# Writing the order of the feed-forward part's first and last stages by hand in a two-layer encoder trunk

## The chip, the cores and the metric

The kernel runs on one core of one Trainium2 chip. The metric is the device time of one execution in microseconds, from the first instruction to the last output byte; lower is better. Times are medians of several executions.

## What is computed

Two layers of an encoder trunk over 768 tokens (512 of one request, 256 of another) of width 1024. In each layer four groups of mixers (attention and recurrences) run between two norms, and then the feed-forward part, which the change is about:

```python
for l in range(DEPTH):
    ...
    x = x + _rms(mix, p['norm_mix_post'][l])
    h = _rms(x, p['norm_ffn_pre'][l])
    f = (jax.nn.silu(h @ p['ffn_w_gate'][l]) * (h @ p['ffn_w_up'][l])) @ p['ffn_w_down'][l]
    x = x + _rms(f, p['norm_ffn_post'][l])
return x
```

The inner width of the feed-forward part is 2816: 22 feature tiles of 128.

## The kernel before

All products are made of fp32 values split into a high and a low part (hi and lo), three matmuls for one product: hi by hi, hi by lo, lo by hi. A split takes two instructions: ACT copies the value into the high tile, and DVE or POOL subtracts it from the value for the low tile. hh and hl are the two parts of the normalised input h, transposed; weights come as raw tiles of 128x1024 by DMA (two buffers of tag raw) and are split into wh and wl tiles.

The feed-forward part of a layer has three stages.

*Head.* `ffn` computes feature tiles 0 and 1 directly: `ffn_up(l, f, s)` (L1261) makes the gate and up products of tile f for request s (s=0 is 512 tokens and 96 matmuls, s=1 is 256 tokens and 48 matmuls) into PSUM tiles fg and fu of tag pS, which has two banks. Then ACT takes tanh (L1270), DVE forms the product in two steps, the first reading fg (L1271), the second reading fu (L1272), ACT writes the high part ah (L1273) and DVE the low part al (L1274). `ffn_sums` (L1199) builds, for each of four row pairs k, sums and differences of the two halves of h (t tiles on POOL and DVE) and splits them (ts tiles); the other 20 feature tiles need them, because these are computed by seven block products of half size in the manner of Strassen. `ffn_sums` ends by overwriting the right half of rows 0 to 3 of hh and hl with a difference (L1226, L1227). Then the down projection of tiles 0 and 1 (`down_mm` L1277, six matmuls into a dn tile of tag pa, two banks; `down_add` L1289, an ACT copy into y for the first pair) runs for 6 token tiles by 2 column halves.

*Units.* `ffn_units` (L1296) handles tiles f = 2 to 21. A unit is seven products p of 12 matmuls (`block_mm` L1249), with additions on DVE (L1304), and the preparation of the next tile's weights: splits called wr, wa, wb and wc, with four sums of raw tiles on POOL (L1317 to L1320) in between. Into the units of pair g the down projection of pair g-1 is placed, six downs to a unit, each added to y on DVE (L1293).

*End.* The 12 downs of the last pair (g = 10) follow, in the order of token tiles `XF_ORDER`, with the post-norm of each token tile (square on ACT, power on POOL, gain on POOL, scale and add on DVE, output DMA) and, in layer 0, the pre-norm and the transposes (hT) for layer 1, whose first matmuls are those of mixer group D (dz).

What sets the order: the program is handed to a scheduler that orders the instructions of each engine by a simulated timeline, except inside `with self.tc.manual_schedule():`, where each engine runs its instructions in the order in which the code issues them. Before the change only `ffn_units` stands inside one; head, end and the group D code are ordered by the scheduler. Each engine is in order: an instruction that waits holds up those behind it.

Of the kernel before, what the change touches and what calls it, by code (L numbers as in the profile page):

```python
# [19 lines left out]
P = 128  # L20
# [65 lines left out]
class Trunk:  # L86
# [585 lines left out]
    def group_d(self, l):  # L672
# [6 lines left out]
        for s, c in ((1, 0), (0, 0), (0, 256)):  # L679
            for (i, u, w), ps in zip(first, bk[1 - s]):  # L680
                self.feat_mm(ps[:, c:c + 256], *w, P, SEQS[s][0] + c, 256)
                if s or c:
                    self.d_part(l, i, u, w, s, ps=ps, mm=False)
                yield 2
# [503 lines left out]
    def mixers(self, l, early):  # L1188
        self.early = early
# [9 lines left out]
    def ffn_sums(self, l):  # L1199
# [5 lines left out]
        units = [self.slot(tag, [P, 2, HT], f"ts{l}_{i}", F32R) for i, tag in enumerate(TS_TAGS)]  # L1205
        cells = [u[:, j] for u in units for j in range(2)]
        cells += [self.slot("z", [P, HT], f"tz{l}_{i}", F32R) for i in range(2)]
        t1s = [self.tmp(f"t1{l}_{j}").rearrange("p (k c) -> p k c", k=2) for j in range(2)]
        self.tt = {}
        for k in range(4):  # L1210
            t1 = t1s[k // 2][:, k % 2]
            t2, t3, t4 = [self.slot("R", [P, 512], f"t{n}{l}_{k}")[:, :HT] for n in (2, 3, 4)]
            for eng, o, r, c in ((A, t1, k, L), (A, t3, k, R), (V, t2, 4 + k, R), (V, t4, 4 + k, L)):
                eng.tensor_tensor(out=o, in0=F(self.hh[:, r, c]), in1=F(self.hl[:, r, c]), op=ALU.add)
            A.tensor_tensor(out=t1, in0=t3, in1=t1, op=ALU.subtract)
            A.tensor_tensor(out=t3, in0=t2, in1=t3, op=ALU.subtract)
            V.tensor_tensor(out=t2, in0=t2, in1=t1, op=ALU.subtract)
            V.tensor_tensor(out=t4, in0=t2, in1=t4, op=ALU.subtract)
            for n, x in ((2, t2), (3, t3), (4, t4)):
                hi, lo = cells.pop(0), cells.pop(0)  # L1220
                S.activation(hi, x, AF.Copy)
                V.tensor_tensor(out=lo, in0=x, in1=F(hi), op=ALU.subtract)
                self.tt[n, k] = hi, lo
        for k in range(4):
            t1, hi = t1s[k // 2][:, k % 2], self.hh[:, k, R]
            S.activation(hi, t1, AF.Copy)  # L1226
            V.tensor_tensor(out=self.hl[:, k, R], in0=t1, in1=F(hi), op=ALU.subtract)  # L1227
# [48 lines left out]
    def down_mm(self, l, g, t, n, act, w):  # L1276
# [18 lines left out]
    def ffn_units(self, l):  # L1295
# [50 lines left out]
        for f in range(2, NF):  # L1346
# [36 lines left out]
            if nxt:  # L1383
                load(nxt, 1)
# [289 lines left out]
```

## Time and profile before

| | |
|---|---|
| median of 3 executions | 2284.88 us (2283.8 to 2291.06) |
| profiled execution | 2280.82 us, span 2279.0 us |
| mean granted clock of TensorE | 0.975 of full |
| PE busy | 2132.7 us, 94% of the span |
| DVE busy | 1608.7 us, 71% |
| ACT busy | 920.4 us, 40% |
| POOL busy | 905.1 us, 40% |

PE is busy in nearly the whole span, so what can be won or lost lies in the short stretches in which it waits. The feed-forward part of layer 0 runs from about 608 to 1132 us, that of layer 1 from about 1744 to 2268 us. Times in the views count from the start of the span.

### The profile page before, as it was taken

What the parts mean: (1) busy time and instruction counts of PE and PEld (TensorE: products, weight loads), DVE (VectorE), ACT (ScalarE), POOL (GpSimd) and SP (SyncE); (2) the same over time, 40 slices, a digit from 0 to 9 for tenths busy, and PEclk for the clock granted to TensorE, in tenths of its full rate; (3) what the DMA queues carried; (4) which work ended last, traced back from release to release, by engine and by line L of the source; (5) the groups of instructions that cost most, each with busy time, mean ns of one, the idle gap of its engine ahead of it and who ended that gap; (6) DMA issues with size and microseconds to landing.
All of it is one profiled execution on the core that took longest, in us unless ns stands there. A gap on an engine that the chain in (4) does not pass through costs nothing.

```text
span 2279.0 us, 43655 instructions
## 1 busy us (share of the span) xinstructions
PE 2132.7 (94%) x17400; PEld 1937.1 (85%) x17400; DVE 1608.7 (71%) x2804; ACT 920.4 (40%) x1863; POOL 905.1 (40%) x733
## 2 busy tenths in 40 slices
PE   7999989989998999999889998899999899999997
PEld 7888878879988999999788888887888789999995
DVE  5597648885766677676766975588857677777666
ACT  4333335665443323332344333455654433323332
POOL 1342313325555454545423432123344545454544
PEclk9999999999999999999999999999999999999999
DMA  4534474345312212122435534643452121221223
GB/s 174 137 104 112 117 216 117 98 132 166 119 32 72 82 58 73 65 68 71 148 101 137 137 83 138 207 121 95 127 172 87 47 76 64 67 73 65 75 65 129
DMA packets 245099, 240.93 MB, mean 106 GB/s; under 512 B 138784, under 2 KB 191904, under 8 KB 244896
## 3 DMA queue, kind: packets, MB, share of 16 engines
q1 hardware_dynamic: 244896, 238.15, 34.3%
q8 instruction: 137, 2.24, 0.4%
q14 instruction: 66, 0.54, 0.1%
HBM read 183.03 MB, written 55.05 MB: 104 GB/s over the span
## 4 chain that ended last, share of the span: by engine, by line
PE 64%; DVE 18%; DMA 7%; issue 4%; POOL 3%; ACT 3%; SPq 1%; DVEq 0%; POOLq 0%; ACTq 0%
PE p L1257 22%; PE dn L1284 13%; PE dz L197 5%; PE op L186 4%; DMA raw<-in_wp_dram 3%; PE za L186 2%; DVE el L461 2%; PE zb L186 2%; DVE nper L463 2%; DVE wlo L168 1%; PE sd L174 1%; PE ob L174 1%; PE fg L197 1%; PE fu L197 1%; PE ptb L767 1%
## 5 line engine op out<-in xcount | busy, mean ns | idle before, releaser
L1245 POOL TENSOR_TENSOR wld<-raw,whd 128x1024 fp32r<-128x1024 f32 x40 | 104.1, 2603 | 345.6 <-ACT whd L1244 345.6
L1293 DVE TENSOR_TENSOR y<-y,dn 128x512 f32<-128x512 f32 x240 | 163.2, 681 | 95.2 <-PE dn L1284 95.0
L1284 PE MATMUL dn<-whd,ah 128*128 128x512 f32 x480 | 192.3, 401 | 18.1 <-DVE y L1293 9.7
L1284 PE MATMUL dn<-whd,al 128*128 128x512 f32 x480 | 191.7, 399 | 1.0 <-DVE al L1446 1.0
L1284 PE MATMUL dn<-wld,ah 128*128 128x512 f32 x480 | 190.3, 396 | 0.0
L168 POOL TENSOR_TENSOR wlo<-raw,whi 128x1024 fp32r<-128x1024 f32 (+1 forms) x48 | 108.6, 2263 | 172.3 <-ACT whi L165 145.5
L1257 PE MATMUL p<-ts,whb 128*128 128x384 f32 x640 | 165.4, 339 | 2.1 <-ACT whb L1244 2.1
L1245 POOL TENSOR_TENSOR wla<-raw,wha 128x1024 fp32r<-128x1024 f32 x40 | 96.0, 2400 | 107.4 <-ACT wha L1244 107.4
L165 ACT ACTIVATE whi<-raw 128x1024 fp32r<-128x1024 f32 (+1 forms) x102 | 99.7, 978 | 90.3 <-DMA raw<-in_wp_dram 34.4
L1304 DVE TENSOR_TENSOR fg<-fg,p 128x384 f32<-128x384 f32 x160 | 87.7, 548 | 60.7 <-PE p L1257 60.3
L1364 ACT ACTIVATE ft<-fg 128x384 f32<-128x384 f32 x80 | 42.0, 525 | 218.2 <-DVE fg L1304 218.2
L1244 ACT ACTIVATE whb<-raw 128x1024 fp32r<-128x1024 f32 x40 | 42.5, 1062 | 208.4 <-POOL raw L1319 208.4
L1257 PEld LDWEIGHTS p<-ts,whb 128*128 128x128 f32 x640 | 116.8, 188 | 9.0 <-ACT whb L1244 2.8
L1284 PEld LDWEIGHTS dn<-whd,ah 128*128 128x128 f32 x480 | 90.8, 189 | 36.3 <-DVE y L1293 15.7
L186 PE MATMUL zc<-whi,hh 128*128 128x256 f32 x384 | 113.8, 298 | 1.5 <-ACT zc L785 0.9
L1368 DVE SCALAR_TENSOR_TENSOR fg<-ft,fg 128x384 f32<-128x384 f32 x80 | 85.3, 1066 | 38.7 <-ACT ft L1364 38.7
L186 PE MATMUL zc<-whi,hl 128*128 128x256 f32 x384 | 111.6, 292 | 0.0
L1284 PEld LDWEIGHTS dn<-whd,al 128*128 128x128 f32 x480 | 90.8, 189 | 24.3 <-DVE al L1446 2.8
L186 PE MATMUL zc<-wlo,hh 128*128 128x256 f32 x384 | 111.4, 292 | 0.0
L1257 PE MATMUL p<-ts,wlb 128*128 128x384 f32 x320 | 108.0, 337 | 1.5 <-DVE wlb L1245 1.5
L1257 PE MATMUL p<-hh,wlc 128*128 128x384 f32 x320 | 107.6, 336 | 1.2 <-DVE wlc L1245 1.2
L1257 PE MATMUL p<-hh,whc 128*128 128x384 f32 x320 | 107.8, 337 | 0.0
(431 smaller groups left out, 7259.4 us busy)
## 6 DMA issues: line engine op xcount, KB each, us to landing
raw<-in_wp_dram SPq DMA_DIRECT2D x184, 512.0 KB
raw<-in_wp_dram SPq DMA_DIRECT2D x38, 384.0 KB
kr<-kd SPq DMA_DIRECT2D x96, 64.0 KB
kr<-kd SPq DMA_DIRECT2D x48, 128.0 KB
x<-xm SPq DMA_DIRECT2D x24, 256.0 KB
xf<-x SPq DMA_DIRECT2D x12, 512.0 KB
gain<-in_bc_dram SPq DMA_DIRECT2D x8, 512.0 KB
bd<-sh SPq DMA_DIRECT2D x8, 512.0 KB
```

The source lines that it names most:

```text
L165: nc.scalar.activation(hi[:, :n], raw[:, :n], AF.Copy)
L168: eng.tensor_tensor(out=lo[:, :n], in0=raw[:, :n], in1=hi[:, :n].bitcast(F32), op=ALU.subtract)
L174: self.nc.tensor.matmul(ps[c], lhsT=lhsT[:, c], rhs=rhs, start=start, stop=stop)
L186: mm(ps, lhsT=a, rhs=b[:, c:c + ncol], start=i == 0, stop=i == tot - 1)
L197: mm(ps, lhsT=a, rhs=b, start=i == 0, stop=i == 3 * NK - 1)
L461: V.tensor_tensor(out=ev, in0=q[:, j + 1:32, j:j + 1].to_broadcast([96, m, j]), in1=q[:, j:j + 1, 0:j].to_broadcast([96, m, j]), op=ALU.mult)
L1245: eng.tensor_tensor(out=lo, in0=x, in1=hi.bitcast(F32), op=ALU.subtract)
L1257: self.nc.tensor.matmul(ps, lhsT=a, rhs=b, start=i == 0, stop=i == 11)
L1284: self.nc.tensor.matmul(ps, lhsT=a[p], rhs=b[q], start=i == 0, stop=i == 5)
L1293: self.nc.vector.tensor_tensor(out=yt, in0=yt, in1=ps, op=ALU.add)
L1304: add = lambda o, x, y, op=ALU.add: V.tensor_tensor(out=o, in0=x, in1=y, op=op)
L1368: V.scalar_tensor_tensor(out=x, in0=th, scalar=1.0, in1=x, op0=ALU.add, op1=ALU.mult)
```

## The change

The code of head and end moves into hand-written functions within `manual_schedule`, and the downs are regrouped. `ffn_up` is split into `up_mm` (matmuls) and `up_gate` (tanh to al), `ffn_sums` now handles one k per call with the final overwriting moved to `ffn_first(k)`, and the weight steps are methods of the same content as before (`w_load`, `w_first`, `w_second`, `w_sums`, `w_third`, `w_fourth`, `down_load`, `down_split`). The units f = 20 and 21 have no downs any more; pairs 9 and 10 are projected together in `ffn_end`, 12 matmuls into one PSUM tile and one addition to y, so each layer has 12 additions on DVE fewer and as many matmuls as before. In layer 0 `ffn_end` loads and splits the first three weight pieces of layer 1, and leaves the norm and transposes of the last two token tiles to be issued among layer 1's first matmuls, which for layer 1 are in hand order as well.

```diff
-FAST = (PIECE_D, PIECE_D + 2, PIECE_D + 6)
-XF_ORDER = (0, 1, 2, 4, 5, 3)
+FAST = (PIECE_D + 2, PIECE_D + 6, PIECE_D)
+XF_ORDER = (4, 5, 0, 1, 2, 3)
...
+    def ffn_head(self, l, ws, tiles):
...
+        self.down_load(l, 0, 0)
+        self.down_load(l, 0, 1)
+        ps = self.up_mm(l, 0, 1, *ws[0])
+        self.ffn_sums(l, 0)
+        self.down_split(l, 0, 0, eng=V)
+        self.w_load(l, 2, 0)
+        self.down_split(l, 0, 1, eng=A)
+        self.w_load(l, 2, 1)
+        self.up_gate(1, *ps, *tiles[0])
+        ps = self.up_mm(l, 1, 0, *ws[1])
+        self.ffn_sums(l, 1)
+        self.w_first(l, 2, ("whi", "wlo"))
+        self.w_second(l, 2)
+        self.ffn_sums(l, 2)
+        self.up_gate(0, *ps, *tiles[1])
+        self.w_sums(2)
+        ps = self.up_mm(l, 1, 1, *ws[1])
+        self.up_gate(1, *ps, *tiles[1])
+        self.w_third(l, 2)
+        act = [t[1:] for t in tiles]
+        due = []
+        todo = {1: [lambda: self.ffn_sums(l, 3)], 4: [lambda: self.ffn_first(0), lambda: self.ffn_first(1)], 6: [lambda: self.ffn_first(2), lambda: self.ffn_first(3)]}
+        for i in range(2 * NT):
+            t, n = i // 2, i % 2
+            due.append(self.down_mm(l, 0, t, n, (act, self.w["d", 0, n])))
+            self.down_add(*due.pop(0))
+            for do in todo.get(i, ()):
+                do()
...
-            downs = [] if g == 1 else [(t, odd) for t in range(NT)]
+            downs = [] if g in (1, NG - 1) else [(t, odd) for t in range(NT)]
...
+        def down(t, n):
+            return self.down_mm(l, NG - 1, t, n, *[(acts[g], self.w["d", g, n]) for g in (NG - 2, NG - 1)])
...
+        for i, t in enumerate(o):
+            xn = pre(o[i - 2]) if i >= 2 and not last else None
+            if i >= 2 and i + 1 < NT:
+                load(o[i + 1])
+            ps = down(t, 0)
+            if i >= 1:
+                post(o[i - 1])
+            sums(t, 0, ps)
+            if xn:
+                for n in range(2):
+                    self.split_T(xn[n], o[i - 2], n)
+            ps = down(t, 1)
+            if i >= 1 and not last:
+                square("p", o[i - 1], x[o[i - 1]])
+                scale("p", o[i - 1])
+            sums(t, 1, ps)
+            square("q", t, self.y[t])
+            if 1 <= i <= 3 and not last:
+                self.early[FAST[i - 1]] = self.ff_split(V, ("whi", "wlo"), f"e{l}_{i}", early.pop(i - 1))
+                early_load(i)
...
         with self.tc.manual_schedule():
-            act, wd = self.ffn_units(l)
+            self.ffn_head(l, ws, tiles)
+            self.late = self.ffn_end(l, self.ffn_units(l))
```

Three places show the moves. In the first, DVE in the head of layer 0: t and ts are the sums of `ffn_sums` (the first number is k), th and al the gate of feature tiles 0 and 1 (fg_1_0 is tile 1, request 0). Before:

```order
L1274 TENSOR_TENSOR al_0_7904<-th_0_7902,ah_0_7903 128x512
L1214 TENSOR_TENSOR t_0_8263<-hh,hl 128x384
L1214 TENSOR_TENSOR t_0_8265<-hh,hl 128x384
L1271 SCALAR_TENSOR_TENSOR th_1_7905<-th_1_7905,fg_1_0_8035 128x512
L1272 SCALAR_TENSOR_TENSOR th_1_7905<-th_1_7905,fu_1_0_8036 128x512
L1274 TENSOR_TENSOR al_1_7907<-th_1_7905,ah_1_7906 128x512
L1271 SCALAR_TENSOR_TENSOR th_0_7902<-th_0_7902,fg_0_1_8138 128x256
L1272 SCALAR_TENSOR_TENSOR th_0_7902<-th_0_7902,fu_0_1_8139 128x256
L1217 TENSOR_TENSOR t_0_8263<-t_0_8263,t_0_8261 128x384
```

After (L1287 and L1288 are the former L1271 and L1272, L1224 to L1232 the former L1214 to L1222):

```order
L1232 TENSOR_TENSOR ts_1_2_8231<-t_1_8229,ts_1_2_8231 128x384
L1232 TENSOR_TENSOR ts_1_4_8232<-t_1_8228,ts_1_4_8232 128x384
L1257 TENSOR_TENSOR wlr_2_8248<-raw_1_0_8116,whr_2_8247 128x512
L1224 TENSOR_TENSOR t_2_8256<-hh,hl 128x384
L1224 TENSOR_TENSOR t_2_8258<-hh,hl 128x384
L1227 TENSOR_TENSOR t_2_8256<-t_2_8256,t_2_8255 128x384
L1228 TENSOR_TENSOR t_2_8258<-t_2_8256,t_2_8258 128x384
L1232 TENSOR_TENSOR ts_2_0_8259<-t_2_8256,ts_2_0_8259 128x384
L1232 TENSOR_TENSOR ts_2_2_8260<-t_2_8258,ts_2_2_8260 128x384
L1232 TENSOR_TENSOR ts_2_4_8261<-t_2_8257,ts_2_4_8261 128x384
L1287 SCALAR_TENSOR_TENSOR th_1_7905<-th_1_7905,fg_1_0_8129 128x512
L1288 SCALAR_TENSOR_TENSOR th_1_7905<-th_1_7905,fu_1_0_8130 128x512
```

The first gate step of tile 1, request 0 stood right behind the first two sums of k=0, and now stands behind all DVE work of k=0, 1 and 2.

The second is POOL at the same place, where the sums of `ffn_sums` and the low parts of the first weights are made. Before, from the last split of the direct tiles' weights on (wlo_43):

```order
L168 TENSOR_TENSOR wlo_43_8348<-raw_43_8345,whi_43_8347 128x1024
L1214 TENSOR_TENSOR t_0_8264<-hh,hl 128x384
L1214 TENSOR_TENSOR t_0_8261<-hh,hl 128x384 x2
L1214 TENSOR_TENSOR t_1_8262<-hh,hl 128x384 x2
L1215 TENSOR_TENSOR t_0_8261<-t_0_8264,t_0_8261 128x384
L1216 TENSOR_TENSOR t_0_8264<-t_0_8263,t_0_8264 128x384
L1214 TENSOR_TENSOR t_1_8281<-hh,hl 128x384
L1215 TENSOR_TENSOR t_0_8261<-t_1_8281,t_0_8261 128x384
L1216 TENSOR_TENSOR t_1_8281<-t_1_8280,t_1_8281 128x384
```

After:

```order
L1226 TENSOR_TENSOR t_0_8093<-t_0_8092,t_0_8093 128x384
L1257 TENSOR_TENSOR wld_0_1_8119<-raw_0_5_8039,whd_0_1_8118 128x1024
L1224 TENSOR_TENSOR t_0_8091<-hh,hl 128x384
L1224 TENSOR_TENSOR t_1_8228<-hh,hl 128x384
L1225 TENSOR_TENSOR t_0_8091<-t_1_8228,t_0_8091 128x384
L1226 TENSOR_TENSOR t_1_8228<-t_1_8227,t_1_8228 128x384
L1257 TENSOR_TENSOR wla_2_8252<-raw_1_1_8122,wha_2_8251 128x1024
L1224 TENSOR_TENSOR t_2_8255<-hh,hl 128x384
L1224 TENSOR_TENSOR t_2_8257<-hh,hl 128x384
L1225 TENSOR_TENSOR t_2_8255<-t_2_8257,t_2_8255 128x384
L1226 TENSOR_TENSOR t_2_8257<-t_2_8256,t_2_8257 128x384
L1327 TENSOR_TENSOR raw_1_1_8122<-raw_1_0_8116,raw_1_1_8122 128x512
```

Two splits of 128x1024 (wld for the downs, wla for tile 2) now stand between the sums of k=0, 1 and 2.

The third is PE at the end of layer 0 (dn_10_4_0 is pair 10, token tile 4, column half 0; ah_18 is the high part of feature tile 18). Before, downs of token tile 0:

```order
L1284 MATMUL dn_10_0_0_12199<-whd_10_0_12037,ah_20_12014 128x512
L1284 MATMUL dn_10_0_0_12199<-wld_10_0_12038,ah_20_12014 128x512
L1284 MATMUL dn_10_0_0_12199<-whd_10_0_12037,al_20_12015 128x512
L1284 MATMUL dn_10_0_0_12199<-whd_10_0_12037,ah_21_12188 128x512
L1284 MATMUL dn_10_0_0_12199<-wld_10_0_12038,ah_21_12188 128x512
L1284 MATMUL dn_10_0_0_12199<-whd_10_0_12037,al_21_12189 128x512
L1284 MATMUL dn_10_0_1_12207<-whd_10_1_12110,ah_20_12014 128x512
L1284 MATMUL dn_10_0_1_12207<-wld_10_1_12111,ah_20_12014 128x512
```

After, from the last product of unit 21 on:

```order
L1269 MATMUL p_21_12071<-hh,wlc_21_11972 128x384
L1301 MATMUL dn_10_4_0_12110<-whd_9_0_11655,ah_18_11630 128x512
L1301 MATMUL dn_10_4_0_12110<-wld_9_0_11656,ah_18_11630 128x512
L1301 MATMUL dn_10_4_0_12110<-whd_9_0_11655,al_18_11631 128x512
L1301 MATMUL dn_10_4_0_12110<-whd_9_0_11655,ah_19_11822 128x512
L1301 MATMUL dn_10_4_0_12110<-wld_9_0_11656,ah_19_11822 128x512
L1301 MATMUL dn_10_4_0_12110<-whd_9_0_11655,al_19_11823 128x512
L1301 MATMUL dn_10_4_0_12110<-whd_10_0_12049,ah_20_11967 128x512
L1301 MATMUL dn_10_4_0_12110<-wld_10_0_12050,ah_20_11967 128x512
L1301 MATMUL dn_10_4_0_12110<-whd_10_0_12049,al_20_11968 128x512
L1301 MATMUL dn_10_4_0_12110<-whd_10_0_12049,ah_21_12093 128x512
L1301 MATMUL dn_10_4_0_12110<-wld_10_0_12050,ah_21_12093 128x512
```

The first downs of the end now take pairs 9 and 10 (ah_18 to ah_21) into one PSUM tile, beginning with token tile 4, and what needs the newest value, ah_21, stands at the end of it.

## Rows read from the trace of the kernel before

**Rows 1.** The page: engine shares, and the chain of waits by engine.

```profile
PE 2132.7 (94%) x17400; PEld 1937.1 (85%) x17400; DVE 1608.7 (71%) x2804; ACT 920.4 (40%) x1863; POOL 905.1 (40%) x733
...
PE 64%; DVE 18%; DMA 7%; issue 4%; POOL 3%; ACT 3%; SPq 1%; DVEq 0%; POOLq 0%; ACTq 0%
```

**Rows 2.** Windows of PE: length, busy (records), granted clock, DMA share, GB/s.

```profile
620.00:632.00 12.00, 12.00 (x92) 1.00 0.01 2
644.50:650.50 6.00, 5.87 (x24) 1.00 0.01 3
```

**Rows 3.** Who PE waits for, 608 to 716 us: total us, times, longest.

```profile
PE dn L1284 <- ACT y L1291: 2.7, 2, 1.8
PE p L1257 <- ACT whr L1244: 2.6, 1, 2.6
PE dn L1284 <- ACT ah L1445: 1.5, 1, 1.5
PE p L1257 <- ACT whb L1244: 1.1, 1, 1.1
PE p L1257 <- DVE wlb L1245: 0.7, 1, 0.7
```

**Rows 4.** Tile p, 640 to 700 us: min/median/max ns, first and last start.

```profile
L1257 PE MATMUL p<-hh,whr x12: 334/334/522, 652.8 to 691.8; 128*128 128x384 f32 x12
```

**Rows 5.** Timeline of DVE, 606 to 660 us: start, length, instruction.

```profile
610.10 1.29 DVE L211 TENSOR_TENSOR hl<-hT,hh 128x512 fp32r<-128x512 f32 x2 [0.27 <-ACT hh L210]
```

**Rows 6.** Groups on POOL, 606 to 720 us: busy, mean ns, idle before.

```profile
L1214 POOL TENSOR_TENSOR t<-hh,hl 128x384 f32<-128x384 f32 x8 | 9.8, 1245 | 18.3 <-DVE ts L1222 16.7 <-DVE hl L211 1.6
L1245 POOL TENSOR_TENSOR wla<-raw,wha 128x1024 fp32r<-128x1024 f32 x4 | 9.5, 2383 | 14.3 <-ACT wha L1244 14.3
...
L1215 POOL TENSOR_TENSOR t<-t,t 128x384 f32<-128x384 f32 x4 | 4.7, 1167 | 0.2
```

**Rows 7.** Groups on ACT, the same stretch and columns.

```profile
L1221 ACT ACTIVATE ts<-t 128x384 fp32r<-128x384 f32 x11 | 5.4, 520 | 5.1 <-DVE t L1217 2.7 <-POOL t L1216 2.3
...
L1244 ACT ACTIVATE whd<-raw 128x1024 fp32r<-128x1024 f32 x2 | 2.1, 1046 | 0.0
```

**Rows 8.** Groups on DVE, the same stretch and columns.

```profile
L1214 DVE TENSOR_TENSOR t<-hh,hl 128x384 f32<-128x384 f32 x8 | 8.1, 1044 | 0.0
...
L1217 DVE TENSOR_TENSOR t<-t,t 128x384 f32<-128x384 f32 x4 | 2.2, 546 | 0.0
...
L1271 DVE SCALAR_TENSOR_TENSOR th<-th,fg 128x512 f32<-128x512 f32 x2 | 1.4, 688 | 4.5 <-ACT th L1270 4.5
```

**Rows 9.** Windows of PE: length, busy (records), granted clock, DMA share, GB/s.

```profile
644.00:648.00 4.00, 3.44 (x15) 1.00 0.02 4
688.50:692.00 3.50, 3.24 (x10) 0.58 0.00 0
1116.00:1120.00 4.00, 3.98 (x12) 0.61 0.00 0
1144.00:1148.00 4.00, 2.76 (x13) 0.50 0.73 209
```

**Rows 10.** Who PE waits for, 1110 to 1165 us (end of layer 0).

```profile
PE hT L206 <- DVE xn L223: 3.3, 2, 2.4
PE hT L206 <- DVE hl L211: 3.1, 1, 3.1
PE dn L1284 <- ACT ah L1445: 2.1, 1, 2.1
```

**Rows 11.** Window of PE over the same stretch, columns as in rows 2.

```profile
1110.00:1165.00 55.00, 41.38 (x223) 0.91 0.38 124
```

**Rows 12.** Who PE waits for, 2240 to 2279 us (end of layer 1).

```profile
PE dn L1284 <- DVE y L1293: 4.3, 3, 1.5
```

**Rows 13.** Timeline of DVE, 2262 to 2279 us.

```profile
2273.16 1.41 DVE L234 SCALAR_TENSOR_TENSOR xf<-yg,q5r,xf 128x512 f32<-128x512 f32 x2 [3.19 <-DMA xf<-x]
2274.49 1.41 DVE L234 SCALAR_TENSOR_TENSOR xf<-yg,q3r,xf 128x512 f32<-128x512 f32 x2
```

More of the change, by code (lines that the diff above doesn't have):

```diff
@@ L678, in group_d @@
               for s, tags in ((1, ("pb", "pb", "pS")), (0, ("pa", "pa", "pS")))]
[L679 to L684, printed above, removed]
+        with self.tc.manual_schedule() if l else nullcontext():
+            one, two, three = self.late if l else [lambda *_a: None] * 3
+            xn = one()
+            for s, c in ((1, 0), (0, 0), (0, 256)):
+                for j, ((i, u, w), ps) in enumerate(zip(first, bk[1 - s])):
+                    self.feat_mm(ps[:, c:c + 256], *w, P, SEQS[s][0] + c, 256)
+                    if j == 0 and (s or c == 0):
+                        xn = (two if s else three)(xn)
+                    if s or c:
+                        self.d_part(l, i, u, w, s, ps=ps, mm=False)
+                    if l == 0:
+                        yield 2
+        if l:
+            yield 18
         (_i, k0, _w), (_i, wd, _w), (_i, r0, _w) = first
@@ L1204, in ffn_sums @@
         L, R = slice(0, HT), slice(HT, TOK)
[L1205 to L1227, printed above, removed]
+        if k % 2 == 0:
+            self.t1s.append(self.tmp(f"t1{l}_{k}").rearrange("p (k c) -> p k c", k=2))
+        t1 = self.t1s[-1][:, k % 2]
+        t2, t3, t4 = [self.slot("R", [P, 512], f"t{n}{l}_{k}")[:, :HT] for n in (2, 3, 4)]
+        cells = []
+        for tag in TS_TAGS[3 * k:3 * k + 3]:
+            u = self.slot(tag, [P, 2, HT], f"ts{l}_{k}_{len(cells)}", F32R)
+            cells += [u[:, j] for j in range(2)]
@@ new lines, in ffn_sums @@
+        if k == 3:
+            cells += [self.slot("z", [P, HT], f"tz{l}_{i}", F32R) for i in range(2)]
+        for eng, o, r, c in ((A, t1, k, L), (A, t3, k, R), (V, t2, 4 + k, R), (V, t4, 4 + k, L)):
+            eng.tensor_tensor(out=o, in0=F(self.hh[:, r, c]), in1=F(self.hl[:, r, c]), op=ALU.add)
+        A.tensor_tensor(out=t1, in0=t3, in1=t1, op=ALU.subtract)
+        A.tensor_tensor(out=t3, in0=t2, in1=t3, op=ALU.subtract)
+        V.tensor_tensor(out=t2, in0=t2, in1=t1, op=ALU.subtract)
@@ L1371, in up @@
                 V.scalar_tensor_tensor(out=x, in0=x, scalar=0.5, in1=u, op0=ALU.mult, op1=ALU.mult)
-            wd = (g - 1, 1) if not odd and g > 1 else (g, 0) if odd else None
+            wd = (g, 0) if odd else (g - 1, 1) if g > 1 else None
+            nwd = (g, 1) if odd else (g, 0)
             if tail:
@@ L1408, in ffn_units @@
             if nxt:
-                second(nxt)
-            else:
-                down_split(g, 1, ("whi", "wlo"))
+                self.w_second(l, nxt)
             add(c12, c12, p)
@@ L1417, in ffn_units @@
             if nxt:
-                first(nxt)
-                sums(nxt)
+                self.w_first(l, nxt)
+                self.w_sums(nxt)
+            else:
+                self.down_split(l, g, 0, ("Q", "Q"))
             add(c22, c12, p)
@@ L1432, in ffn_units @@
             if nxt:
-                third(nxt)
-            nwd = (g, 0) if not odd else (g, 1)
-            if nxt:
-                down_load(*nwd)
+                self.w_third(l, nxt)
+                self.down_load(l, *nwd)
+            else:
+                self.down_split(l, g, 1, ("Q", "raw"))
             settle(1)
@@ L1507, in run @@
         for l in range(L):
-            self.mixers(l, early if l == 0 else {})
+            self.mixers(l)
             self.ffn(l)
```

214 lines of the change are left out of this document (128 added, 86 removed).

## The prediction

> **What bounds the kernel now.** I read the page first: PE is busy in 94% of the span and carries 64% of the chain that ends last [rows 1]. The change leaves the number of matmuls as it is, so it can win or lose only where PE waits, at four places: the head and the end of the feed-forward part, in two layers. Second I read who PE waits for at these places. In the head of layer 0 the reader is to see several short waits, the longest 2.6 us, for the first raw weights of a unit, and 2.7 us in two pieces for the copies of dn into y [rows 3]. At the end of layer 0 the waits are for the normalised tile and its transposes, 3.3 and 3.1 us [rows 10]; at the end of layer 1, 4.3 us for the additions to y [rows 12]. [...] Last I read what single instructions of DVE, ACT and POOL take in the head [rows 6 to 8], since the change writes those engines' order by hand, and an instruction in the wrong place holds up all that is behind it.
>
> **The head of layer 0, walked.** PE's order is the same up to the last transposes. From there on:
>
> The products of tile 0 for request 1 now come first and need the last hl, which DVE finishes at 610.10 + 1.29 = 611.4 us [rows 5]. Before, PE went on at 609.6 with tile 1, which did not need it. Cost 1.7 us.
>
> These are 48 matmuls. 92 recorded ones took 12.00 us [rows 2], so 48 take 6 and 96 take 12 (a few records are missing); PE is done at 617.4.
>
> The next products, tile 1 for request 0 (96 matmuls), need the two banks of tag pS back, that is the gate steps of the products just made (L1287, L1288). The tanh for them stands on ACT behind three ts copies of 0.52 and two wd copies of 1.05 [rows 7], and the ts copies wait for the sums of k=0, which take POOL two additions of 1.245 and two subtractions of about 1.167, 4.8 us [rows 6], from 610.9 to 615.7. So DVE subtracts at 616.3, the ts copies end near 618, the wd copies at 620.0, and the gate step gives the bank back at 620.6. PE waits 3.2 us.
>
> The 96 matmuls run to 632.6. The last 48 direct products (tile 1, request 1) again need both banks, whose gate step on DVE stands behind all sums of k=1 and k=2 and behind wlr. What it waits for is a chain on POOL: wld from 620.0 (2.4, taken equal to wla [rows 6]) to 622.4; sums of k=1, 4.8, to 627.2; then ACT's three ts copies, the copies whr (half of 1.05) and wha, 3.1 us, to 630.3; wla 2.4, to 632.7; sums of k=2, 4.8, to 637.5; then a subtraction of 0.55, three ts copies of 0.52, a tanh (an ACT step like a ts copy, a little longer) and the gate step of 0.69 [rows 7, 8], about 3.4 us, to 641. PE waits 8.4 us. This is the largest term. Bounds: no wait at all if this chain ran 8 us faster, 11 if DVE's subtractions beside POOL cost 1.04 instead of 0.55 [rows 8]. I take 8.4, since each link has its own row.
>
> Then 6 us of products and 12 downs of 6 matmuls. 24 of these took 5.87 us [rows 2], so a down takes 1.47 and the 12 take 17.6. In them the copies of dn into y stand on ACT behind the ts copies of k=3, which wait for POOL once more; I estimate 2.5 us of waiting, against the 2.7 us for y that stand there now [rows 3]; bounds 0 and 4. Behind an idle stretch of 8 us the clock will be low; behind the 2.6 us one it was 0.58 over 3.5 us, a loss of 0.42 x 3.5 = 1.5 [rows 9], which I take here too.
>
> Tile 2 starts at 641 + 6 + 17.6 + 2.5 + 1.5 = 668.6. It starts at 652.8 now [rows 4]. **Head of layer 0: +16 us.** In layer 1 the order is the same, except that POOL has a split of a direct weight, 2.4 us, ahead of a norm; I take **+17**.
>
> **What the head gives back.** The weights of tile 2 are ready while the downs run, so units 2 and 3 need not wait for whb, 1.1 us [rows 3], nor for its three low parts, each a shorter wait than that; I put them at 1.6 together. The wait of 2.6 us for whr of tile 4 [rows 3] arises because two raw buffers serve three loads for each unit; this loop starts about 3 us earlier against the unit, so the wait goes, and the low clock behind it (0.58 over 3.5 us [rows 9], some 1.5 us) with it. The wait for ah, 1.5 us, stays: it is a chain of gate and split behind the last product of a unit, with the same cover. Gain 1.1 + 1.6 + 2.6 + 1.5 = 6.8; bounds 2 (whr is merely late elsewhere) and 9. **-7 us in each layer.**
>
> **Units 20 and 21.** Without downs a unit is PE time of its own, and the downs are made later: nothing moves in the sum. The 12 additions on DVE per layer lie beside PE work and cost nothing before; the cover is the unit itself. If the weight preparation of unit 21 outlasted the shorter unit 20, it would cost up to 1 us.
>
> **End of layer 0.** PE is busy for 41.4 of 55 us [rows 11], so it waits 13.6, of which the ah wait of 2.1 [rows 10] stays. The low clock in two windows of 4 us loses 0.39 x 4 and 0.50 x 4, 3.6 us [rows 9]. Together 17 to 18. But the early splits of three weight pieces stand on DVE and ACT, 1.05 on ACT [rows 7] and at most the 2.4 of POOL's like split [rows 6] on DVE, ahead of the norms of the token tiles; the transposes of a tile wait for its norm, and PE is in order, so downs that could run stand behind the transposes. I walk two waits near 3 us, the ah wait, some smaller ones, and the clock behind them: 15 us remain. **-3 us**, bounds 0 (as many waits as now) and -14 (all but the ah wait and its clock).
>
> **End of layer 1.** There is no pre-norm and no early split. A down of 12 matmuls, 2.9 us, is longer than the addition that it has to cover, so the 4.3 us for y [rows 12] go. The last token tile's input is loaded early, so DVE's wait of 3.2 us for that transfer goes, and only one token tile is scaled at the end instead of two in turn: 2274.49 - 2273.16 = 1.3 us [rows 13]. That is 8.8; I leave 0.8 for a longer last addition chain. **-8 us**, bounds -2 and -11.
>
> **Sum:** 16 + 17 - 7 - 7 - 3 - 8 = +8 us, on the profiled execution of 2280.82 us (span 2279.0). That execution is 4.1 us below the median of the runs, 2284.88, to which the same difference applies: 2284.88 + 8 = **2293 us**.
>
> **Contention, weighed.** The group L1214 on DVE, run beside POOL, takes 1.04 us on the mean, the group L1217, of the same shape and mostly without POOL, 0.55 [rows 8]. The sum above uses a mixture. [...]
>
> **Rivals.**
> *The gates are free in time.* If POOL's sums of k=1 and 2 and the two splits overlap better than I walk them, and the gate of tile 1 is done before PE needs the bank, the long wait is gone. It decides at 632.6: the chain must be 8 us shorter. For it: POOL is busy only 40% of the span [rows 1], and it waited 16.7 us for ts tiles in this stretch before [rows 6]. Against it: POOL runs 19 us back to back here, and every link is a wait in program order. Each head is then 16 - 8.4 - 1.5 - 3 (the small waits are cut in part) = +3, less 7; heads together -8 instead of +19, and the ends -11 as above: about **2268 us**, faster.
> *The end pays in full.* The early weights of layer 1 leave PE without waits but for ah: -14 at layer 0 instead of -3. For it: the downs are now 2.9 us long and cover more. Against it: DVE was the releaser of nearly all waits there [rows 10] and has gained work. Sum +19 - 14 - 8 = -3: **2282 us**, no change.
> *DVE doubles beside POOL.* About eight subtractions of the chain in each head at 1.04 instead of 0.55, 4 us a head, with the clock: +16 in all, **2301 us**.
>
> **How the numbers follow.** Two executions of this kernel can be told apart from about 0.3%, 7 us. My forecast (2288 to 2298) has a chance of 0.40, the free gates 0.18, the end in full with like compensations 0.27, the doubled subtractions 0.15. Faster by over 0.3% (under 2278): the free gates and little else, 0.20. Within 0.3% (to 2291.7): the end in full and the low part of the forecast, 0.30. Slower: 0.50. The range takes in the rivals' points but leaves out the tails below 2268 and above 2304. The likeliest sign, slower, has its own range of 2288 to 2304.
>
> **What would show it.** Right: PE waits of about 3 and 8 us for a DVE gate step (L1287) at some 617 and 633 us, and the same in layer 1; a low clock behind the second; tile 2 starting near 668 us; no wait for whr of tile 4; the last store of layer 1 some 4 us sooner after the last down than now. Wrong: tile 2 starting before 658 us, or PE waits in the head under 4 us, which would be the free gates; the end of layer 0 without transposes that wait, which would be the end in full; waits inside the units 5 to 19, of which I expect no change.

## The result and the profile after

| | before | after |
|---|---|---|
| median of the runs | 2287.97 us (2283.8 to 2291.78, 4 runs) | 2305.52 us (2302.98 to 2308.17, 4 runs) |
| ratio, 95% interval | 1 | 1.0077 [1.0052, 1.0102] |
| profiled execution, span | 2280.82, 2279.0 us | 2308.17, 2306.4 us |
| mean granted clock | 0.975 | 0.969 |

The change makes the kernel 17.6 us slower, twice what was forecast and 1.5 us above the range. (The forecast of 2293 started from a median of 2284.88 us over three executions; with the fourth it is 2287.97. So 3.1 of the 12.5 us by which 2305.52 exceeds 2293 lie in the start.) The two traces differ by 27.4 us: the traced execution of before lies under all its timed runs, that of after at the top of its own. The stretches below show where the time is; the medians say how much. To which stretches the 10 us between the two differences belong is not known.

The page of the kernel after, engine shares and chain (before: [rows 1]):

```profile
PE 2139.6 (93%) x17400; PEld 1944.7 (84%) x17400; DVE 1600.5 (69%) x2780; ACT 919.3 (40%) x1863; POOL 900.3 (39%) x733
...
PE 58%; DVE 18%; DMA 7%; POOL 6%; ACT 5%; issue 4%; SPq 1%; POOLq 0%; DVEq 0%; ACTq 0%
```

As many matmuls as before. POOL's share of the chain has doubled: it now sits in a chain that PE waits for. Who PE waits for in the kernel after, 604 to 716 us (before: [rows 3]):

```profile
PE fg L197 <- DVE th L1287: 14.3, 2, 11.1
PE dn L1301 <- ACT ah L1490: 3.0, 1, 3.0
PE dn L1301 <- ACT y L1308: 2.0, 1, 2.0
PE p L1269 <- DVE wlr L1257: 0.4, 1, 0.4
```

The two gate waits of the forecast are there. In the PE timeline they stand ahead of the products of tile 1, request 0, and of tile 1, request 1 (start, length, instruction, idle before):

```profile
616.21 0.58 PE L197 MATMUL fg<-hh,whi 128*128 128x256 f32 x1 [3.22 <-DVE th L1287]
...
641.46 0.58 PE L197 MATMUL fg<-hh,whi 128*128 128x256 f32 x1 [11.05 <-DVE th L1287]
```

Windows of PE over those two sets of products (columns as in [rows 2]), and tile p, whose first start is the end of the head (before: [rows 4]):

```profile
616.20:630.50 14.30, 14.20 (x96) 0.80 0.24 75
641.50:649.50 8.00, 8.00 (x50) 0.73 0.00 0
```

```profile
L1269 PE MATMUL p<-hh,whr x12: 334/334/440, 668.3 to 700.3; 128*128 128x384 f32 x12
```

The granted clock is 0.50 behind both waits, the one of 3.2 us too (616.20 to 621.50 and 641.50 to 645.50 us), and 1.00 later on (622.10 to 630.40 and 646.00 to 649.10): PE's matmuls of 128x256 start 0.21 us apart at first, and 0.12 us apart later on. So 96 products take 14.2 us and 48 take 7.7; at 0.119 us each they take 11.4 and 5.7, so 4.8 us are lost together. The head, from its last transposes (605.07) to tile 2 (668.26), lasts 63.2 us; before it was 44.0.

**Where the time went, stretch by stretch.** Both kernels were traced a second time (the last experiment). The ends of layer 0 and 1 are counted without the 12 downs of 1.47 us (17.6 us) that moved there from the units, and the units with them. In before's layer 1, 42 direct products stand ahead of the last transposes, so the border of its mixers is set 5.3 us earlier, where as much work is done (5767 matmul records against 5766).

| stretch | forecast | first traces | second traces |
|---|---|---|---|
| head, layer 0 and 1 | +16, +17 | +19.2, +19.5 | +18.7, +18.8 |
| units 2 to 21, layer 0 and 1 | -7, -7 | -3.7, -4.1 | -3.0, -3.9 |
| end of layer 0, to the first dz matmul of the second projection | -3 | -3.8 | -3.4 |
| end of layer 1, to the last byte | -8 | -7.1 | -5.8 |
| up to the head of layer 0 | 0 | -3.8 | -1.2 |
| layer 1's mixers | 0 | +11.2 | +7.2 |
| sum | +8 | +27.4 | +27.4 |

The 1.47 us are the forecast's. In the timelines the matmuls of a down start 0.233 us apart at a granted clock of 1.00, which makes 1.40 us for a down; by that figure 0.8 us move from each end to the units before it (units -4.5 and -4.9, ends -3.0 and -6.3 in the first traces). And executions differ: PE's matmuls up to the head of layer 0 come in the same order in all 14 traces of this document, and that stretch takes between 605.1 and 613.2 us.

**Why 11 us and not 8.** Timelines of DVE and of POOL in the kernel after, ahead of the second wait:

```profile
633.32 1.60 DVE L1227 TENSOR_TENSOR t<-t,t 128x384 f32<-128x384 f32 x1 [4.00 <-POOL t L1226]
634.95 1.51 DVE L1228 TENSOR_TENSOR t<-t,t 128x384 f32<-128x384 f32 x1
636.38 4.42 DVE L1232 TENSOR_TENSOR ts<-t,ts 128x384 fp32r<-128x384 f32 x3
640.73 0.67 DVE L1287 SCALAR_TENSOR_TENSOR th<-th,fg 128x512 f32<-128x512 f32 x1
```

```profile
632.29 0.99 POOL L1226 TENSOR_TENSOR t<-t,t 128x384 f32<-128x384 f32 x1
633.24 1.26 POOL L1327 TENSOR_TENSOR raw<-raw,raw 128x512 f32<-128x512 f32 x1
634.58 1.46 POOL L1328 TENSOR_TENSOR raw<-raw 128x512 f32<-128x512 f32 x1
636.12 1.46 POOL L1329 TENSOR_TENSOR raw<-raw,raw 128x512 f32<-128x512 f32 x1
637.66 1.46 POOL L1330 TENSOR_TENSOR raw<-raw,raw 128x512 f32<-128x512 f32 x1
639.09 2.57 POOL L1224 TENSOR_TENSOR t<-hh,hl 128x384 f32<-128x384 f32 x2
```

POOL finished the sums of k=2 at 633.28, and the walk had 637.5 less the 3.8 us by which this trace reaches the head sooner: that chain was right. But the four raw sums (w_sums) follow on POOL at once, and beside them each of DVE's five steps (two differences, three low parts) takes 1.5 us, where the bound was 1.04 [rows 8]. The walk went over one DVE step of 0.55 and three copies on ACT; undisturbed, DVE's five steps take no longer (2.8 us in experiment 5), but here they end last: the products that the gate step reads were done at 630.41 and their tanh on ACT at 637.92, and the step started at 640.73, behind the low parts ahead of it on DVE. From the sums to the end of the gate step it is 8.1 us, not 3.4. PE, at a granted clock of 0.80 over the 96 products, came 1.6 us later, hence 11.05. The gate step L1287, which reads fg in PSUM, keeps its 0.67 beside POOL.

**The ends.** Who PE waits for after the units, 1100 to 1165 us (before: [rows 10]), then 2250 to 2307 us (before: [rows 12]):

```profile
PE hT L206 <- DVE xn L1535: 7.8, 3, 3.1
PE dn L1301 <- ACT ah L1490: 5.0, 1, 5.0
...
PE dn L1301 <- ACT ah L1490: 4.9, 1, 4.9
```

The waits for y at the very end are gone, as forecast. The wait for ah after unit 21, 2.1 us before, is 5.0 in layer 0, and in layer 1 it is 4.9, where before had:

```profile
PE dn L1284 <- ACT ah L1445: 1.2, 1, 1.2
```

DVE and POOL in unit 21 of the kernel after:

```profile
1102.29 2.40 DVE L1385 TENSOR_TENSOR fu<-fu 128x384 f32<-128x384 f32 x1
1104.72 2.63 DVE L1418 SCALAR_TENSOR_TENSOR fg<-fg,fu 128x384 f32<-128x384 f32 x1
...
1108.20 0.54 DVE L1385 TENSOR_TENSOR fg<-fg,p 128x384 f32<-128x384 f32 x1
```

```profile
1101.88 5.06 POOL L1257 TENSOR_TENSOR wld<-raw,whd 128x1024 fp32r<-128x1024 f32 x2 [8.87 <-ACT whd L1256]
```

The two splits for the downs run on POOL here, and two DVE steps beside them take 2.4 and 2.6 us. The last product ends at 1104.35; the addition that needs it (1108.20) stands behind them.

### The profile page after: what moved, and what is told of

The parts are those of the page before. It is cut to its first block, busy times and chain, and to the rows that moved or that the text cites. A ratio compares the mean times of both kernels' runs of the same rounds, so it can differ in the third digit from the quotient of the medians.

```text
span 2306.4 us, 43646 instructions
## 1 busy us (share of the span) xinstructions
PE 2139.6 (93%) x17400; PEld 1944.7 (84%) x17400; DVE 1600.5 (69%) x2780; ACT 919.3 (40%) x1863; POOL 900.3 (39%) x733
## 4 chain that ended last, share of the span: by engine, by line
PE 58%; DVE 18%; DMA 7%; POOL 6%; ACT 5%; issue 4%; SPq 1%; POOLq 0%; DVEq 0%; ACTq 0%
PE p L1269 20%; PE dn L1301 14%; PE dz L197 5%; DMA raw<-in_wp_dram 4%; PE op L186 3%; PE zb L186 2%; PE za L186 2%; DVE el L461 2%; DVE nper L463 2%; PE sd L174 1%; POOL wla L1257 1%; PE ob L174 1%; PE zc L186 1%; DVE wlo L168 1%; PE ptb L776 1%
## 5 line engine op out<-in xcount | busy, mean ns | idle before, releaser
L1301 PE MATMUL dn<-whd,ah 128*128 128x512 f32 x528 | 212.6, 403 | 20.5 <-ACT ah L1490 15.8
L1301 PE MATMUL dn<-whd,al 128*128 128x512 f32 x528 | 211.2, 400 | 0.5 <-DVE al L1491 0.5
L1301 PE MATMUL dn<-wld,ah 128*128 128x512 f32 x528 | 210.9, 399 | 0.0
L1310 DVE TENSOR_TENSOR y<-y,dn 128x512 f32<-128x512 f32 x216 | 147.3, 682 | 89.3 <-PE dn L1301 89.2
L1269 PE MATMUL p<-ts,whb 128*128 128x384 f32 x560 | 146.4, 343 | 0.0
L1301 PEld LDWEIGHTS dn<-whd,ah 128*128 128x128 f32 x528 | 101.0, 191 | 39.5 <-ACT ah L1490 17.6
L1301 PEld LDWEIGHTS dn<-whd,al 128*128 128x128 f32 x528 | 100.7, 191 | 26.4 <-DVE al L1491 2.4
L1301 PEld LDWEIGHTS dn<-wld,ah 128*128 128x128 f32 x528 | 101.1, 192 | 16.2
L1269 PEld LDWEIGHTS p<-ts,whb 128*128 128x128 f32 x560 | 103.6, 190 | 5.5
L1269 PE MATMUL p<-hl,whc 128*128 128x384 f32 x320 | 107.6, 336 | 0.0
```

What stands on the lines that cost most here:

```text
L1269: self.nc.tensor.matmul(ps, lhsT=a, rhs=b, start=i == 0, stop=i == 11)
L1301: self.nc.tensor.matmul(ps, lhsT=a[p], rhs=b[q], start=i == 0, stop=i == 6 * len(pairs) - 1)
L1310: self.nc.vector.tensor_tensor(out=yt, in0=yt, in1=ps, op=ALU.add)
```

## The experiments

Theory A: the hand-written head loses what the change loses, the rest wins some. The edits are against the kernel after.

**1. The head back to the scheduler.** Everything else of the change stays.

```diff
+        self.ffn_head(l, ws, tiles)
         with self.tc.manual_schedule():
-            self.ffn_head(l, ws, tiles)
+            self.ffn_prime(l)
```

(ffn_head then has products, gates, sums and downs in the plain order of the kernel before; ffn_prime issues the weight steps of tile 2.)

> Undoes one part: the head (direct products, sums, first downs) goes back to the scheduler in the code order of before; units 20 and 21 without downs, the 12-matmul downs and the hand-written end stay. Theory A (the hand-written head is the loss, the end is a gain): in the trace the head took 19 us longer in layer 0 and 25 in layer 1, of which the units gave back 4 each; without that, what is left is the gain of the ends, 4 + 7 + 4 less some 3 us at the units without downs: 9 to 13 us under before, about 2276 to 2280. Theory B (the end and its early splits cost as much as the head, the head's losses being partly clock): 0 to 6 us above before.

Measured 2279.01 us (2273.92 to 2283.39), ratio 0.9965 [0.9947, 0.9982]; no wait for L1287 is left. The head by hand, with what it gives back, costs 26.5 us by these medians, and what else the change does gains 8.1, somewhat less than A's 9 to 13. (The 25 us for layer 1 in the two texts counts from the last transposes, ahead of which before has done 42 products; by equal work it is the 19.5 of the table.)

**2. The end, the units' splits and layer 1's first matmuls as before, the head by hand.**

```diff
-FAST = (PIECE_D + 2, PIECE_D + 6, PIECE_D)
+FAST = (PIECE_D, PIECE_D + 2, PIECE_D + 6)
...
-            downs = [] if g in (1, NG - 1) else [(t, odd) for t in range(NT)]
+            downs = [] if g == 1 else [(t, odd) for t in range(NT)]
...
-            self.late = self.ffn_end(l, self.ffn_units(l))
+            acts = self.ffn_units(l)
...
```

(The downs and norms of the kernel before follow as they stood.)

> The other half alone: the hand-written head stays, units 20 and 21 have their downs again, and end, early splits and the start of layer 1 are as before. Theory A: before + 19 + 25 less 4 and 4 given back in the units, 25 to 36 us above before, thus slower than the whole change by about 10: 2313 to 2324. Theory B: the head's part is half of the 18 us, 2294 to 2300, faster than the whole change.

Measured 2308.72 us (2304.66 to 2317.04), ratio 1.0098 [1.0074, 1.0122]. That is under A's figure of 2313 to 2324 (2308 to 2318 with 19.5 us in place of 25) and over B's of 2294 to 2300. The head by hand costs 21.6 us here, against 26.5 in the first experiment, so B falls; but this kernel is only 3 us slower than the whole change, and the two intervals overlap. What else the change does is thus worth some 3 to 8 us. One reason why it is not more stands in the table: the ends win some 10 us, and layer 1's mixers lose 7 to 11 again. In this kernel's trace, with the old end, the mixers took 556.8 us (experiment 10 takes that up).

**3. The gate earlier in the queues.** It undoes the suspected order and leaves the work.

```diff
         self.ffn_sums(l, 1)
+        self.up_gate(0, *ps, *tiles[1])
+        ps = self.up_mm(l, 1, 1, *ws[1])
         self.w_first(l, 2, ("whi", "wlo"))
         self.w_second(l, 2)
         self.ffn_sums(l, 2)
-        self.up_gate(0, *ps, *tiles[1])
-        self.w_sums(2)
-        ps = self.up_mm(l, 1, 1, *ws[1])
         self.up_gate(1, *ps, *tiles[1])
+        self.w_sums(2)
```

> One move within the hand-written head: the gate of tile 1, request 0, and the products of tile 1, request 1, stand right behind the sums of k=1, ahead of the first weight splits of tile 2 and the sums of k=2; nothing else is changed. Theory A1 (the place of the gate in the order makes the 11 and 12 us waits): both waits go to under 3 us, the low clock behind them too, so 18 to 26 us under the changed kernel, 2280 to 2288, about as before. Theory A2 (POOL's chain of sums and splits is the bound of the head whatever the order): the wait moves to the downs or to tile 2's first products, and the time falls by under 8 us, to 2298 or more.

Measured 2303.52 us (2301.07 to 2304.94), ratio 1.0070 [1.0055, 1.0085]: 2 us, no gain to speak of, as A2 has it. PE's waits in the head of this kernel, and POOL's timeline:

```profile
PE dn L1301 <- ACT y L1308: 11.9, 2, 11.6
PE fg L197 <- DVE th L1287: 3.2, 1, 3.2
```

```profile
629.84 1.02 POOL L1226 TENSOR_TENSOR t<-t,t 128x384 f32<-128x384 f32 x1
640.32 2.50 POOL L1257 TENSOR_TENSOR wla<-raw,wha 128x1024 fp32r<-128x1024 f32 x1 [9.47 <-PE fg L197]
```

The 11 us wait has gone from the gate to the first downs. ACT's copies whr and wha now stand behind the tanh of products that PE has yet to make, so POOL idles for 9.5 us, k=2 and 3 come later, and the copies of dn into y stand behind them. So the gate's place alone does not make the time: with the rest of this order, the chain through ACT, POOL and DVE is late wherever PE next needs it.

**4. The splits of unit 21 moved to where POOL is free**: one to the start of the unit, one behind the last gate.

```diff
                 self.down_load(l, g, 1)
+                self.down_split(l, g, 0, ("Q", "Q"))
...
-            else:
-                self.down_split(l, g, 0, ("Q", "Q"))
...
-            else:
-                self.down_split(l, g, 1, ("Q", "raw"))
...
         settle()
+        self.down_split(l, NG - 1, 1, ("Q", "raw"))
```

> One move in unit 21: the split of the first down weights of pair 10 stands at the unit's start, where POOL is idle, and that of the second behind the unit's last gate; nothing else is changed. Theory C (two POOL splits in unit 21 slow DVE beside them, 2.4 and 2.6 us for steps of 0.55, and so the last gate comes late): the wait for ah behind unit 21 falls from 5.0 and 4.9 us to about 2, and with the low clock behind it the time falls by 5 to 9 us, to 2297 to 2301. Theory D (a unit without downs is too short for DVE's work whatever POOL does): the wait stays over 4 us, time within 2 us of the changed kernel.

Measured 2302.29 us (2300.91 to 2304.8), ratio 1.0067 [1.0052, 1.0082]. The two DVE steps and the wait, in the trace of this kernel:

```profile
1109.83 0.56 DVE L1385 TENSOR_TENSOR fu<-fu 128x384 f32<-128x384 f32 x1
1110.42 0.56 DVE L1418 SCALAR_TENSOR_TENSOR fg<-fg,fu 128x384 f32<-128x384 f32 x1
```

```profile
PE dn L1301 <- ACT ah L1487: 2.5, 1, 2.5
```

With POOL quiet beside them the steps are back at 0.56 us and the wait at 2.5, in both layers. The cause of the wait is shown. The time falls by 3.2 us, less than the 5 to 9 expected, and the intervals of the two kernels overlap; experiment 8, where the medians with the same move are 4 to 5 us lower, points the same way.

**5. POOL quiet beside the chain of k=2**: the raw sums come after the sums of k=3, whose POOL additions go to DVE.

```diff
-        self.w_sums(2)
...
-        self.w_third(l, 2)
...
-        todo = {1: [lambda: self.ffn_sums(l, 3)], 4: [lambda: self.ffn_first(0), lambda: self.ffn_first(1)], 6: [lambda: self.ffn_first(2), lambda: self.ffn_first(3)]}
+        todo = {1: [lambda: self.ffn_sums(l, 3, V), lambda: self.w_sums(2), lambda: self.w_third(l, 2)], 4: [lambda: self.ffn_first(0), lambda: self.ffn_first(1)], 6: [lambda: self.ffn_first(2), lambda: self.ffn_first(3)]}
```

> In the hand-written head POOL has nothing to do while DVE makes the differences of k=2: the four raw sums of tile 2 and the third split stand behind the sums of k=3, and the first two additions of k=3 are on DVE instead of POOL. PE's order and the gate's place are as in the changed kernel. Theory A3 (the 11 us wait is longer than forecast because DVE's seven steps of k=2 take 1.5 us each beside POOL's raw sums instead of 0.55): these steps go to about 0.55, the wait before the products of tile 1, request 1, falls from 11.1 and 12.3 us to 6 to 8, and the time falls by 6 to 10 us unless the later raw sums hold up tile 2. Theory A4 (they are slow for another reason, such as their operands): the steps stay above 1.2 us and the wait over 10.

Measured 2306.27 us (2300.88 to 2306.93), ratio 1.0078 [1.0057, 1.0099]. DVE's steps of k=2 and PE's waits in the head of this kernel:

```profile
635.02 0.56 DVE L1228 TENSOR_TENSOR t<-t,t 128x384 f32<-128x384 f32 x1 [4.00 <-POOL t L1227]
635.61 0.56 DVE L1229 TENSOR_TENSOR t<-t,t 128x384 f32<-128x384 f32 x1
636.17 1.62 DVE L1233 TENSOR_TENSOR ts<-t,ts 128x384 fp32r<-128x384 f32 x3
...
653.58 1.51 DVE L1229 TENSOR_TENSOR t<-t,t 128x384 f32<-128x384 f32 x1
```

```profile
PE fg L197 <- DVE th L1288: 9.5, 2, 6.3
PE dn L1302 <- ACT y L1309: 5.3, 1, 5.3
```

Five steps in 2.8 us instead of 7.5, and the gate wait 4.8 us shorter, as A3 has it: the contention was real, and A4 falls. But the raw sums now run beside the steps of k=3, which take 1.5 us in their turn, and the wait for y grows from 2.0 to 5.3. The work was moved along the same chain: the head still lasts 63.9 us, and the 6 to 10 us that A3 expected did not come.

**6. Another hand order**: tile 1 first, each gate ahead of the next sums, k=1 behind the last direct products, k=2 and 3 among the downs.

```diff
-        ps = self.up_mm(l, 0, 1, *ws[0])
+        ps = self.up_mm(l, 1, 0, *ws[1])
         self.ffn_sums(l, 0)
...
+        self.up_gate(0, *ps, *tiles[1])
+        ps = self.up_mm(l, 0, 1, *ws[0])
         self.up_gate(1, *ps, *tiles[0])
...
+        todo = {1: [lambda: self.up_gate(1, *ps, *tiles[1])], 3: [lambda: self.ffn_sums(l, 2)],
+                7: [lambda: self.ffn_sums(l, 3), lambda: self.w_sums(2), lambda: self.w_third(l, 2)],
+                11: [lambda k=k: self.ffn_first(k) for k in range(4)]}
```

> Another hand order of the head: products of tile 1, request 0, first (as the scheduler had them), each gate ahead of the next sums, sums of k=1 behind the last direct products, sums of k=2 and 3 among the downs. Theory A (the hand-written head loses by its order alone, and the same work fits behind PE in another one): no wait for a gate over 2 us, and 20 to 30 us under the changed kernel: 2275 to 2285. Rival (DVE, POOL and ACT have more work in the head than PE covers, and a wait of 8 us or more for y, ts or wla takes the place of the others): 2295 or more.

Measured 2284.87 us (2278.06 to 2289.88), ratio 0.9991 [0.9978, 1.0003]. The gate waits are gone; of the waits in the head the longest are for y:

```profile
PE dn L1301 <- ACT y L1308: 5.3, 2, 3.1
```

The head is 48.2 us, against 63.2 in the kernel after and 44.0 before. The time is 20.7 us under the changed kernel, as theory A has it. So it is not hand order as such that costs most of the time, but putting POOL's work for k=1 and 2 and two splits ahead of the gate on which PE's last direct products wait, instead of beside the downs, which need none of it.

**7. The early weight splits of layer 1 behind the pre-norm.**

```diff
             xn = pre(o[i - 2]) if i >= 2 and not last else None
+            if 2 <= i <= 4 and not last:
+                self.early[FAST[i - 2]] = self.ff_split(V, ("whi", "wlo"), f"e{l}_{i}", early.pop(i - 2))
+                early_load(i - 1)
...
-            if 1 <= i <= 3 and not last:
-                self.early[FAST[i - 1]] = self.ff_split(V, ("whi", "wlo"), f"e{l}_{i}", early.pop(i - 1))
-                early_load(i)
```

> One move in the hand-written end of layer 0: each early split of a weight piece of layer 1 stands behind the pre-norm of the token tile that it stood ahead of; nothing else is changed. Theory F (the early splits on DVE hold up the norms, and these the transposes and downs): the first two waits for xn, 2.2 and 2.5 us, fall under 1, and the time falls by 3 to 6 us. Rival (the norm chain itself is late, or the splits are then late for the products of layer 1): within 2 us of the changed kernel.

Measured 2308.93 us (2307.2 to 2312.2), ratio 1.0099 [1.0082, 1.0116]. The waits for xn fall from 7.8 to 4.4 us, so the splits do hold up the norms, and the end of layer 0 is 2.6 us shorter in the trace; the time is not, against theory F's 3 to 6 us.

**8. Experiments 1 and 4 together**, in two sets of runs.

> The head left to the scheduler as in the first experiment, and the down splits of pair 10 moved as in the fourth. If both act by themselves: 2279 less 3, 2274 to 2278, 10 to 13 us under the kernel before.

> The same kernel as the combination (head by the scheduler, the down splits of unit 21 moved), run once more as the partner of the next one and to see whether its gain stands. Expected if it stands: ratio to the kernel before 0.993 to 0.997, about 2272 to 2280 us. If the first result was luck of the runs: 0.998 or more.

Measured 2274.79 us at first (ratio 0.9949 [0.9929, 0.9969]), and in the second set 2274.1 us (2268.17 to 2281.33, 11 runs), ratio 0.9959 [0.9942, 0.9976]. The gain stands, inside both expectations.

**9. Experiments 1, 4 and 7 together.**

> The combination with the early weight splits of layer 1 put behind the pre-norm as well. Theory F (these splits hold up the norms and cost time, which the run on the slow head only hid): the xn waits of the end fall from 7.8 to about 4 us in all and the time is 3 to 4 us below the partner's. Rival F2 (what the norms win the splits lose, since layer 1's first matmuls then wait for the early weights or for y): the xn waits fall, the time is within 2 us of the partner's, and the stretch from the last product to the first dz matmul is no more than 2 us shorter.

Measured **2270.13 us** (2268.25 to 2277.11), ratio 0.9939 [0.9918, 0.9961], 4 us under its partner, as theory F has it; the two intervals overlap, so these 4 us alone are not certain. Its waits for xn:

```profile
PE hT L206 <- DVE xn L1527: 4.5, 3, 3.1
```

From the last product to the first dz matmul of the second projection it takes 78.5 us, its partner 84.2. This version beats the kernel before by 0.6% and the change by 1.5%.

**10. Both kernels traced again.**

> The kernel before, unchanged, for a second trace. In the first one the same work of layer 1's mixers (first dz matmul of the second projection to the last transposes, 5767 matmul records) took 559.7 us, in the kernel after 570.9. Theory V (most of the 11 us is a difference between executions, of the granted clock above all): this trace has 564 us or more. Rival V2 (the hand order of layer 1's first matmuls makes the mixers slower): it has 562 or less.

> The whole change, unchanged, for a second trace. Theory V: the mixers of layer 1 take 561 to 572 us. Rival V2: 568 or more. Theory A, whatever they take: the two heads again 62 to 64.5 us each, the gate waits again 10 to 13 us, and the ah wait behind unit 21 near 5 us, since these come from the order and not from the execution.

One execution each: 2282.74 and 2310.11 us. Windows of PE over the same work of layer 1's mixers, first the kernel after (first trace), then, in a fence each, before (first and second trace) and the kernel of experiment 2 with the old end:

```profile
1187.45:1758.30 570.85, 530.32 (x5766) 0.95 0.46 131
```

```profile
1179.54:1739.20 559.66, 521.54 (x5767) 0.96 0.47 135
```

```profile
1183.72:1742.71 558.99, 518.34 (x5768) 0.97 0.47 135
```

```profile
1194.75:1751.56 556.81, 518.63 (x5767) 0.97 0.47 134
```

Theory V falls by its own figure: before's mixers take the same 559 us again. V2's figure of 568 for the second trace of after was too high (566.2), but its direction holds in every trace: 556.8 to 559.7 us in the three with the old end, 562.3 to 571.1 in the eleven with the new one. In the windows above PE is busy for longer in the kernel after (530.3 us against 518.3 to 521.5), at a lower granted clock (0.95 against 0.96 and 0.97). Executions differ all the same: in nine of the eleven PE does the mixers' matmuls in one and the same order, and these alone lie between 562.3 and 570.9 us, so the 7 to 11 us are not known closely. Against the old end PE's order differs from the 23rd of these matmuls on. Which part does it (the order of the token tiles, the early weights, or the order that the scheduler then finds) was not tried apart.

Theory A's figures: heads of 63.1 and 63.0 us, as expected; all gate waits of this trace, both layers:

```profile
PE fg L197 <- DVE th L1287: 31.1, 4, 13.6
```

The longest passes the 13 expected; the wait for ah behind unit 21 of layer 0 was 5.7.

## Why the prediction was right in kind and wrong in size

The change is slower, and mainly for the reason walked: a gate step on DVE that stands behind a chain through POOL. Three steps failed: the price of DVE's steps and of the clock in the heads (+38.7 us instead of +33), what the units give back (-7.8 instead of -14), and the premise that only "four places", the heads and the ends, can win or lose: layer 1's mixers, at nothing in the sum, lost 7 to 11 us.

- **Head, +16 and +17: right in place and kind, short by 2 to 3 us each.** The walked 3.2 us wait measured 3.22, the copies into y 2.0 for 2.5, the late hl about 1.1 for 1.7. Two links failed. "A subtraction of 0.55 ... about 3.4 us" for the steps behind POOL's sums was 8.1, since they ran at 1.5 us beside POOL (shown by experiment 5), and the wait became 11.05 for 8.4. And the clock took 4.8 us for 1.5, since it was 0.50 for 5.3 us behind the 3.2 us wait as well. An error the other way hid part of that: the window of 92 records [rows 2] holds 11 matmuls of the first downs too, so 12 and 6 us for the products were too long, as was 1.47 for a down; at a granted clock of 1.00 it is 11.4, 5.7 and 1.40, some 2 us less for the head. The rival "DVE doubles beside POOL" is thus what happened in this chain, at nearly three times instead of the two of [rows 8].
- **"-7 us in each layer": -4 in the table.** Two things are mixed there. Where only the head differs, the units are 4.8 and 5.2 us shorter with the hand-written head (the kernel after against experiment 1) or 5.5 and 6.5 (experiment 2 against before), so the head gives back 5 to 6 us; units 20 and 21 take the rest (next point). The waits for whb, for low parts and for whr did go (0.4 for wlr is left). But "the wait for ah, 1.5 us, stays" was wrong: it is 3.0 in both layers, and the granted clock behind it is 0.50 for some 3 us (710.7 to 713.9 and 1864.4 to 1867.5 us), where it was 0.58 over 3.5 us behind whr [rows 9], so that the 1.5 for the clock came to nothing. In the kernel after, DVE itself stands for whr ahead of that gate:

```profile
697.85 1.00 DVE L1257 TENSOR_TENSOR wlr<-raw,whr 128x512 fp32r<-128x512 f32 x1 [3.14 <-ACT whr L1256]
```

 That the lateness moved from PE into DVE's queue is one reading, and was not tried alone. Layer 1 of experiment 1, with the scheduler's head, speaks against it, since it has both waits:

```profile
PE dn L1301 <- ACT ah L1484: 3.0, 1, 3.0
PE p L1269 <- ACT whr L1256: 2.5, 1, 2.5
```

 Why the ah wait is 3.0 stays open.
- **Units 20 and 21, "nothing moves in the sum": wrong.** In experiment 1, whose head is as long as before's, the units take 1.1 us more than before's less the moved downs (0.3 with downs of 1.40). And the wait for ah behind them grew by 2.9 us in layer 0 and 3.7 in layer 1, since moved splits on POOL stretched DVE's last additions (shown by experiment 4). The walk of the end let that wait stay as it was.
- **Ends, -3 and -8: right in sum** (-3.8 and -7.1), partly by luck. The transposes that wait are there as walked, three, at 7.8 us in all; the waits for y at the very end went, and the last step of DVE ends 4.2 us after the last down instead of 8.2. But the grown waits for ah were not in the walk, and what made up for them was not followed.
- **Layer 1's mixers were not in the sum at all.** They belong to the change, since the end decides what layer 1 starts with; they lost 7 to 11 us, about as much as the ends gained. What in the change does it stays open.
- **Rivals.** "The gates are free" (whose sum, -8 and -11, makes 2266 us, not 2268) and "the end pays in full" did not come. Of the signs named for a right reading, the wait for whr was gone, the last store came some 4 us sooner, and the waits of 3 and 8 us were 3 and 11. Tile 2 started at 668.3 us where 668 was named, but that is luck: this trace came to the head 3.8 us sooner than before's; in the second trace tile 2 starts at 673.6.

## What to carry to other kernels

Before moving a POOL instruction by hand, ask which DVE step with both inputs in SBUF will run beside it: in this case such a step lasted about as long as the POOL instruction beside it (1.5 or 2.5 us), not its own 0.56. When a wait is removed by order alone, follow the whole chain behind it (here ACT, POOL, DVE): experiments 3 and 5 moved the wait and kept most of its length, and only work taken from ahead of PE's last direct products shortened it (experiments 1 and 6). And count the stretch after the changed one: here layer 1's mixers lost about as much as the ends won.

## What the runs showed of the hardware

The size of the contention was not expected. A DVE step of 128x384 with both inputs in SBUF takes 0.56 us alone (experiments 4 and 5), 1.5 to 1.6 beside POOL instructions of 128x512 that run back to back, and 2.4 to 2.6 beside one of 128x1024; the gate step of 128x512, which has one of its inputs in PSUM, keeps its 0.67 (0.69 before [rows 8]). In the timelines above the two engines go in step: POOL's raw sums start 1.3 to 1.5 us apart, DVE's steps end some 1.5 us apart, and the first two of them end 0.4 us after a POOL instruction (634.92 and 636.46 against 634.50 and 636.04). What couples the two no run here shows.
